# One written order on ScalarE and VectorE for the stage of the three pairs with meta tokens, with other banks and buffers

## The chip, the cores and the metric

The kernel runs on one core of a Trainium2 chip. A core has TensorE (PE in the profile, with PEld for its weight loads), VectorE (DVE), ScalarE (ACT), GpSimd (POOL) and SyncE (SP, which issues the transfers). Each engine works through its own list of instructions in order; semaphores tie the lists together. The metric is the time of one execution on the device in microseconds. The kernel before takes 1217.13 us, the median of three runs (1213.55 to 1217.62).

## The reference, cut to what matters

One block of a hybrid encoder: 1024 tokens of width 1024, with 16 learned meta tokens in front, through a norm, one wide projection `w_in`, two mixers, gates, an output projection and a squared-ReLU MLP.

```
z = u @ w_in                               # u: normed rows, meta tokens first
a, q, k, v, r, lr, ga, gb = split(z)       # widths 512, 256, 256, 512, 512, 16, 1024, 1024
p = multiscale_pool(a)                     # per group of 128: mean over 2, 4, 8 or 16 rows, minus the row
p = einsum(p, w_pool_mix) * pool_scale     # 128x128 per group
log_a = log_sigmoid(lr @ w_gate_up + b_gate) / 16
o = gla_chunked(q, k, v, log_a)            # gated linear attention in chunks of 64
m = sigmoid(ga) * (p @ w_pool_out) + sigmoid(gb) * (rmsnorm(o) * silu(r) @ w_gla_out)
```

Only `a`, `k`, `v` and `lr` are needed for the meta tokens too; that is why the stage that makes `a` and `k` works on 1040 columns and stands apart from the later projections.

## The kernel before, in words

All large products run in fp32 split in two: every operand is kept as a high part (fp32r) and a low remainder, and `mm3` (lines 285 to 287) issues high x high, high x low and low x high into the same PSUM bank. So each weight block needs a copy on ACT (the high part) and a subtraction on DVE (the low part) before PE can use it. With those three matmuls for each product PE is the busiest engine by far.

**The stage of the three pairs** is `first_products` (from line 750). A *pair* is two blocks of 128 columns of `w_in`: pair 0 is groups 2 and 3 of `a`, pair 1 groups 0 and 1, pair 2 is `k`. A pair is computed by a seven-product scheme (P1 to P7 on sums of blocks, as in Strassen's method), so the stage has 21 products; their order is the list `ORDER_2` (line 744), and n below is the place in it (n = 0 is P1 of pair 0, n = 20 is P3 of pair 2). For each n the loop issues the product (`product`, line 823), then the split of the weights for product n + 4 into one of four slots (`ready_for`, line 755; lines 789 and 790 are its ACT copy and DVE subtraction), and then what the table `beside` names for that place. Sums of weight blocks are made by POOL (line 673). Results leave PSUM through `put` and `copy` (lines 819 and 820).

PSUM has eight banks: tag `sc` (two banks, products of pairs 0 and 2), `gs` (two banks, pair 1), `y2` (two banks, always taken as one buffer) and `z` (two buffers of one bank). `two("sc")` and `two("gs")` give the same tile each time, while each `two("y2")` and `bank("z")` takes the next buffer of its pool and so waits until the last user has been read out.

**The work beside the products** is threefold.
- `lr_turn` (line 414), at n = 0: the low-rank columns `lr` (16 for each row of tokens) are transposed by PE, 16x16 for the meta tokens into a `z` bank and four 128-row blocks each into the first and the second half of `gs`. `stacked` copies each to two places on ACT (lines 416, 417) and writes the remainder on DVE (418).
- `decays(p)` (line 618), for each half of the heads: two matmuls (621) into `y2`, then Identity, Abs, Exp and Ln on ACT and one step on DVE over 1024 columns (609 to 616), in the buffers `c` (two of its four) and `dt`, an Exp (625) and a store to `decay_dram` (626). The same follows for the 16 meta columns (630) into the small tile `metab`.
- `mix_sums(g)` and `mix_products(g)`: the pooling sums of group g on DVE (645, 648) in the two `s` buffers, the split of the mixed rows into `ph` (649 on ACT, 650 on DVE), six matmuls with the 128x128 mixing weight (285 to 287 in `ph,mw`), a scaled copy out (658) into the same `s` buffer, and a store to `pm_dram` (659). They run for groups 2, 3, 1, 0.

Two things outside matter here. The **meta state** (`meta_state`, lines 1131 to 1141) uses `metab`: small DVE steps and one ACT Exp for each p, and loads of `metab` from `k_dram` (1136) that need the meta columns of `k` to be stored (817). And the **next stage**, `pairs_of_projections`, frees the right stack of SBUF (`right.pop_to(0)`) and pushes its own tiles, `fs` first: so `fs` (128 x 2 x 512) takes the memory that `dt` (128 x 2 x 512, the first tile pushed by this stage) had. POOL writes the weight sums for the fourth product of that stage (P5 of its first pair) into `fs` (line 984).

**What sets the order.** PE, POOL and SP instructions, and ACT and DVE instructions outside the first stage, are put in order by the tile framework's scheduler, from its own estimates; `tc.keep_in_program_order` pins single ones. The first stage is already written out by hand inside `tc.manual_schedule(engines={ACT, DVE, SP})`. SP issues every transfer of the main queue in one list, and a transfer whose data are not ready holds back those behind it.

Of the kernel before, what the change touches and what calls it, by code (L numbers as in the profile page):

```python
# [10 lines left out]
ACT = mybir.ActivationFunctionType  # L11
# [111 lines left out]
def kernel(  # L123
# [30 lines left out]
    def bank(tag):  # L154
        if tag == "sc":
            sc_n[0] += 1
            return two("sc")[:, sc_n[0] % 2]
        return psp[tag].tile([P, 512], F32, name=f"b_{tag}", tag=tag)

    def two(tag):  # L160

        if tag in ("sc", "gs"):
            if tag not in wide:
                wide[tag] = psp[tag].tile([P, 2, 512], F32, name=f"b_{tag}", tag=tag)
            return wide[tag]
        return psp[tag].tile([P, 2, 512], F32, name=f"b_{tag}", tag=tag)
# [247 lines left out]
    def lr_turn():  # L414
        def stacked(to, b):
            act.activation(to[:16], b, ACT.Copy)
            act.activation(to[64:80], b, ACT.Copy)
            dve.tensor_tensor(to[32:48], b, f32(to[:16]), ALU.subtract)

        b = bank("z")  # L420
        pe.transpose(b[:16, :16], S["lrtok"][:16, 8], ident[:16, :16])
        stacked(S["lr"][:, SEQ : SEQ + META], b[:16, :16])
        for h, c in enumerate(halves()):
            b = two("gs")[:, h]
            for t in range(4):
                pe.transpose(b[:16, t * P : (t + 1) * P], S["lrtok"][:, 4 * h + t], ident)
            stacked(S["lr"][:, c], b[:16])
# [190 lines left out]
    def decays(p):  # L618
        b, up = two("y2"), S["gu"][:, p * P : (p + 1) * P]
        for half, c in enumerate(halves()):  # L620
            pe.matmul(b[:, half], up, S["lr"][:, c], start=True, stop=True)
        y, t = S["c"][:, :2], S["dt"]
        yield from log_decay(b, y, t, p)
        yield
        act.activation(y, y, ACT.Exp, scale=1.0 / TAU)
        nc.sync.dma_start(decay_dram[p].rearrange("h p t -> p h t"), y)
        if p:
            act.activation(gnorm, gnorm, ACT.Copy, scale=0.5)
        b = two("y2")[:, 0, :META]
        pe.matmul(b, up, S["lr"][:, SEQ : SEQ + META], start=True, stop=True)  # L630
        for _ in log_decay(b, metab[:, META_LOG[p]], metab[:, 4], p):
            pass
        if p:
            tc.keep_in_program_order(act.preload_act_table_set("exp_and_others"))

    pooled = {}

    def mix_sums(g, eng=dve):
        a, w, e = pooled[g], WINDOWS[g], SEQ + META
        cur, k = a, 1  # L640
        while k < w:
            c = META - (w - 2 * k)
            dst = nxt("s")
            for lo, hi in ((c, e),) if eng is dve else ((c, HALF), (HALF, e)):
                eng.tensor_tensor(dst[:, lo:hi], cur[:, lo:hi], cur[:, lo - k : hi - k], ALU.add)
            cur, k = dst, 2 * k
        pp = S["pp"] = nxt("s")
        dve.scalar_tensor_tensor(pp[:, :SEQ], cur[:, META:e], 1.0 / w, a[:, META:e], ALU.mult, ALU.subtract)
        act.activation(S["ph"][:, 0], pp[:, :SEQ], ACT.Copy)
        dve.tensor_tensor(S["ph"][:, 1], pp[:, :SEQ], f32(S["ph"][:, 0]), ALU.subtract)  # L650

    def mix_products(g, tag):
        wb = (S["mw"][:, 0, g], S["mw"][:, 1, g])
        b = two(tag)
        for h, c in enumerate(halves()):
            mm3(b[:, h], 1, lambda i: wb, lambda i: (S["ph"][:, 0, c], S["ph"][:, 1, c]))
        o = S["pp"][:, :SEQ].rearrange("p (h c) -> p h c", h=2)
        act.activation(o, b, ACT.Copy, scale=pscale[:, g : g + 1])
        nc.sync.dma_start(pm_dram[g].rearrange("h p t -> p h t"), o)

# [89 lines left out]
    def first_products(wb):  # L750
# [4 lines left out]
        def ready_for(n):  # L755

            if n >= len(ORDER_2):
                if n > len(ORDER_2):
                    S["first"].append(next(S["pw"]))
                return  # L760
            p, i = ORDER_2[n]
            hi, lo = slots[(0, 2, 1, 3)[n % 4]]
            if i == 0 and p in ("P1", "P2"):
                return
            if i == 0:
                a = S["sums"][p]
            else:
                a11, a12, a21, a22 = (first_raw[i, u][:, k : k + 4] for u in range(2) for k in (0, 4))
                f, s, s5 = quad(fs), quad(s3), quad(S["c"][:, 3])
                if p == "P1":  # L770
                    a = a11
                    in_halves(s5, a21, a22, ALU.add)
                elif p == "P2":
                    a = a12
                elif p == "P6":
                    a = f
                    in_halves(f, s5, a11, ALU.subtract)
                elif p == "P5":
                    a = s5
                    in_halves(s, a11, a21, ALU.subtract)  # L780
                elif p == "P7":
                    a = s
                elif p == "P4":
                    a = a22
                else:
                    a = f
                    in_halves(f, a12, f, ALU.subtract)
            hi, lo = quad(hi), quad(lo)
            act.activation(hi, a, ACT.Copy)
            dve.tensor_tensor(lo, a, f32(hi), ALU.subtract)  # L790
# [74 lines left out]
        def mixing_weights():  # L865
            r = nxt("s")[:, :HALF]
            nc.sync.dma_start(r.rearrange("p (g e) -> p g e", g=4), w_pool_mix.rearrange("g c e -> c g e"))
            r = r.rearrange("p (g e) -> p g e", g=4)
            tc.keep_in_program_order(act.activation(S["mw"][:, 0], r, ACT.Copy))
            dve.tensor_tensor(S["mw"][:, 1], r, f32(S["mw"][:, 0]), ALU.subtract)  # L870

        ready_for(1)
# [5 lines left out]
        S["ph"] = right.push("ph", [P, 2, SEQ], F32R)  # L878
        S["mw"] = right.push("mw", [P, 2, 4, P], F32R)
        S["first"] = []  # L880
        logs = iter(())
        beside = {
            0: lr_turn,
            6: lambda: (mixing_weights(), mix_sums(2)),
            9: lambda: (mix_products(2, "y2"), mix_sums(3)),
            13: lambda: (mix_products(3, "y2"), mix_sums(1)),
            17: lambda: (mix_products(1, "gs"), mix_sums(0)),
            20: lambda: mix_products(0, "gs"),
        }
        for n in range(len(ORDER_2)):  # L890
            product(n)
            ready_for(n + 4)
            if n == 6:
                for u in range(2):
                    load_pair_block(2, u)
            if n == 11:
                first_pair()
            beside.get(n, lambda: None)()
            if n in (3, 10):
                logs = decays(n // 10)  # L900
            next(logs, None)

    step(one, first_products, W1, [w_cols(FIRST[0])])

# [1009 lines left out]
```

## Time and profile before

| | |
|---|---|
| median of three runs | 1217.13 us (1213.55 to 1217.62) |
| the profiled execution | 1217.57 us, of which the span from first to last instruction is 1215.8 us |
| mean granted TensorE clock | 0.994 of full |
| PE busy | 1192.8 us, 98% of the span |
| DVE, ACT, POOL busy | 853.9, 579.1 and 103.5 us |

Times inside the execution count from the start of the span. The stage of the three pairs runs from about 73 us (its first product) to about 156 us (the first product of the next stage). In a row of the timeline stand the start, the duration, engine, line, operation, output and inputs with their shapes; in square brackets stands how long the engine had been idle before and what released it. A row of the waits says who waited for what: total us, times, the longest. A row of the stretches gives, for each engine, the busy time in a stretch, and then the granted PE clock, the share of the transfer engines and their rate. Consecutive matmuls overlap in the records, so PE's pace is read from start to start.

### The profile page before, as it was taken

How to read it: one execution, taken by the hardware profiler on the slowest of the kernel's cores; microseconds unless marked ns; L12 is line 12 of the kernel's file. 1: busy time of each engine (PE TensorE's matmuls, PEld its weight loads, DVE VectorE, ACT ScalarE, POOL GpSimd, SP SyncE). 2: the span in 40 equal slices, each digit the busy share in tenths (PEclk: the TensorE clock that was granted, in tenths of full speed). 3: DMA queues.
4: the chain of work that ended last, by engine and by line, in shares of the span. 5: the costliest groups of instructions: out<-in, count | busy, mean ns of one | idle time of the engine just before them, and what ended most of it. 6: DMA issues, size and time to landing. Idle time of an engine off the chain costs nothing.

```text
span 1215.8 us, 18350 instructions
## 1 busy us (share of the span) xinstructions
PE 1192.8 (98%) x6775; PEld 991.2 (82%) x6775; DVE 853.9 (70%) x1392; ACT 579.1 (48%) x1006; POOL 103.5 (9%) x121
## 2 busy tenths in 40 slices
PE   9988999999999999999999999999999999999997
PEld 7978888777788888788878888888888888888886
DVE  6666856665677569725887667676675887887686
ACT  7546544444456224314655455454454444444544
POOL 0223233323320000000000000000000000000000
PEclk9989999999999999999999999999999999999999
DMA  8232343435347977911245444454479973332532
GB/s 245 65 79 87 105 116 121 147 105 164 98 140 240 342 241 245 317 51 70 104 140 168 145 163 156 130 164 146 167 243 315 337 241 101 96 98 93 174 95 87
DMA packets 151001, 192.79 MB, mean 159 GB/s; under 512 B 12088, under 2 KB 85616, under 8 KB 150912
## 3 DMA queue, kind: packets, MB, share of 16 engines
q1 hardware_dynamic: 150752, 191.56, 48.6%
q8 instruction: 53, 0.87, 0.3%
q14 instruction: 36, 0.29, 0.1%
q10 hardware_dynamic: 160, 0.07, 0.0%
HBM read 128.66 MB, written 62.93 MB: 158 GB/s over the span
## 4 chain that ended last, share of the span: by engine, by line
PE 67%; DVE 3%; DMA 1%; issue 1%; ACT 1%; SPq 0%; DVEq 0%
PE b_oa L287 5%; PE b_oa L286 5%; PE b_oa L285 5%; PE b_y L285 4%; PE b_y L287 4%; PE b_y L286 4%; PE b_mm L285 4%; PE b_mm L287 4%; PE b_mm L286 4%; PE b_ob L287 4%; PE b_ob L286 4%; PE b_ob L285 4%; PE b_z L286 3%; PE b_z L285 3%; PE b_z L287 3%; PE b_sc L285 2%
## 5 line engine op out<-in xcount | busy, mean ns | idle before, releaser
L285 PE MATMUL b_z<-th,w1h 128*128 128x512 f32 x240 | 95.7, 399 | 0.0
L286 PE MATMUL b_z<-tl,w1h 128*128 128x512 f32 x240 | 94.5, 394 | 0.4 <-DVE tl L1583 0.4
L287 PE MATMUL b_z<-th,w1l 128*128 128x512 f32 x240 | 94.2, 393 | 0.0
L285 PE MATMUL b_sc<-th,w1h 128*128 128x512 f32 (+1 forms) x232 | 89.8, 387 | 0.5 <-ACT u2p L1697 0.5
L948 ACT ACTIVATE w1h<-raw 128x512 fp32r<-128x512 f32 x103 | 64.0, 622 | 53.4 <-PE b_y L286 23.1
L286 PE MATMUL b_sc<-tl,w1h 128*128 128x512 f32 (+1 forms) x232 | 89.3, 385 | 0.0
L287 PE MATMUL b_sc<-th,w1l 128*128 128x512 f32 (+1 forms) x232 | 88.9, 383 | 0.0
L948 ACT ACTIVATE w1h<-fs 128x512 fp32r<-128x512 f32 x81 | 51.1, 631 | 66.8 <-PE b_y L286 34.9
L949 DVE TENSOR_TENSOR w1l<-raw,w1h 128x512 fp32r<-128x512 f32 x103 | 70.7, 688 | 16.5 <-ACT w1h L948 16.5
L949 DVE TENSOR_TENSOR w1l<-fs,w1h 128x512 fp32r<-128x512 f32 x81 | 56.3, 695 | 20.8 <-ACT w1h L948 20.7
L948 ACT ACTIVATE w1h<-bt 128x512 fp32r<-128x512 f32 x46 | 29.1, 632 | 70.9 <-issue 43.9
L1773 DVE TENSOR_TENSOR bt<-w,w 128x512 f32<-128x512 f32 x80 | 54.6, 683 | 1.0 <-DMA w<-in_w_ff_dram 0.9
L286 PEld LDWEIGHTS b_z<-tl,w1h 128*128 128x128 f32 x240 | 45.8, 191 | 10.3 <-DVE tl L1583 0.8
L285 PEld LDWEIGHTS b_z<-th,w1h 128*128 128x128 f32 x240 | 45.8, 191 | 10.2 <-issue 0.4
L287 PEld LDWEIGHTS b_z<-th,w1l 128*128 128x128 f32 x240 | 45.7, 190 | 10.0
L285 PEld LDWEIGHTS b_sc<-th,w1h 128*128 128x128 f32 x232 | 43.5, 188 | 10.2 <-ACT u2p L1697 1.0
L287 PEld LDWEIGHTS b_sc<-th,w1l 128*128 128x128 f32 x232 | 43.6, 188 | 8.9
L286 PEld LDWEIGHTS b_sc<-tl,w1h 128*128 128x128 f32 x232 | 43.6, 188 | 8.6
L285 PE MATMUL b_mm<-wo,th 128*128 128x512 f32 x128 | 50.4, 394 | 0.0
L287 PE MATMUL b_mm<-wo,tl 128*128 128x512 f32 x128 | 49.9, 390 | 0.0
L286 PE MATMUL b_mm<-wo,th 128*128 128x512 f32 x128 | 49.8, 389 | 0.0
L285 PE MATMUL b_y<-wo,w1h 128*128 128x512 f32 x128 | 49.8, 389 | 0.0
(513 smaller groups left out, 3402.9 us busy)
## 6 DMA issues: line engine op xcount, KB each, us to landing
hf_dram<-h SPq DMA_DIRECT2D x112, 256.0 KB, 2.1
raw<-hf_dram SPq DMA_DIRECT2D x112, 256.0 KB, 2.6
w<-in_w_ff_dram SPq DMA_DIRECT2D x64, 256.0 KB, 4.8
raw<-in_w_in_dram SPq DMA_DIRECT2D x18, 512.0 KB, 4.7
raw<-in_w_ff_dram SPq DMA_DIRECT2D x16, 512.0 KB, 4.1
rawx<-in_w_ff_dram SPq DMA_DIRECT2D x16, 512.0 KB, 4.0
rawp<-in_w_in_dram SPq DMA_DIRECT2D x14, 512.0 KB, 4.3
xs<-in_x_dram SPq DMA_DIRECT2D x8, 512.0 KB, 4.8
```

Source lines behind the costliest of these rows:

```text
L285: pe.matmul(ps, ah, bh, start=first and i == 0, stop=False, skip_group_check=more)
L286: pe.matmul(ps, ah, bl, start=False, stop=False, skip_group_check=more)
L287: pe.matmul(ps, al, bh, start=False, stop=last and i == n - 1, skip_group_check=more)
L948: act.activation(hi, a, ACT.Copy)
L949: dve.tensor_tensor(lo, a, f32(hi), ALU.subtract)
L1773: dve.tensor_tensor(bt, w, S["w2"][q[3:]][:, i], ALU.add if q[2] == "+" else ALU.subtract)
```

## The change

The ACT and DVE instructions of the stage are put inside `tc.manual_schedule`, so that they stand in the order in which the loop issues them; the table `beside` is rewritten to say after which product each step goes. To make such a table possible, `decays` yields once more (between the Exp with its store and the meta columns), and the split of the mixed rows leaves `mix_sums` for a function `mix_parts` of its own. Two single pins are dropped. Four places change what memory a step uses:
- `lr_turn` puts the 16x16 transpose into `y2`, the first four blocks into a `z` bank and only the second four into `gs`;
- `mix_products` copies its result into `dt` instead of the `s` buffer of the sums, so the four stores to `pm_dram` read `dt`;
- the loads of pair 2 are issued by the table (n = 6), and the first loads of the next stage too (n = 11), at the places where they were.

```
-        b = bank("z")
+        b = two("y2")[:, 0]
         pe.transpose(b[:16, :16], S["lrtok"][:16, 8], ident[:16, :16])
...
-            b = two("gs")[:, h]
+            b = two("gs")[:, 0] if h else bank("z")
...
         nc.sync.dma_start(decay_dram[p].rearrange("h p t -> p h t"), y)
+        yield
...
-            tc.keep_in_program_order(act.preload_act_table_set("exp_and_others"))
+            act.preload_act_table_set("exp_and_others")
...
+    def mix_parts():
+        pp = S["pp"]
         act.activation(S["ph"][:, 0], pp[:, :SEQ], ACT.Copy)
         dve.tensor_tensor(S["ph"][:, 1], pp[:, :SEQ], f32(S["ph"][:, 0]), ALU.subtract)
...
-        o = S["pp"][:, :SEQ].rearrange("p (h c) -> p h c", h=2)
+        o = S["dt"]
         act.activation(o, b, ACT.Copy, scale=pscale[:, g : g + 1])
         nc.sync.dma_start(pm_dram[g].rearrange("h p t -> p h t"), o)
...
-            0: lr_turn,
-            6: lambda: (mixing_weights(), mix_sums(2)),
-            9: lambda: (mix_products(2, "y2"), mix_sums(3)),
...
+            0: (lr_turn,), 3: (log(0),), 4: (log(0), mixing_weights), 5: (log(0),), 6: (log(0), sums(2), more_loads),
+            7: (log(0),), 8: (mix_parts,), 9: (log(0),), 10: (products(2, "y2"), sums(3)), 11: (mix_parts, first_pair),
+            12: (log(1),), 13: (log(1),), 14: (log(1),), 15: (log(1), products(3, "y2"), sums(1)),
+            16: (log(1), mix_parts, log(1)), 17: (products(1, "gs"), sums(0)), 18: (mix_parts,), 20: (products(0, "gs"),),
         }
-        for n in range(len(ORDER_2)):
-            product(n)
-            ready_for(n + 4)
...
+        with tc.manual_schedule(engines={mybir.EngineType.Activation, mybir.EngineType.DVE}):
+            for n in range(len(ORDER_2)):
+                product(n)
+                ready_for(n + 4)
+                for do in beside.get(n, ()):
+                    do()
```

Before, `decays(0)` started after n = 3 and `decays(1)` after n = 10, one step per product; the mixing went in after n = 6, 9, 13, 17 and 20. Outside the stage the order stays, apart from a few weight splits at the start of the next one. Line numbers of the changed kernel are 3 or 4 higher behind the first edits.

On PE, at the start of the stage, `lr_turn` stands behind P1 of pair 0 (`b_sc`) and ahead of P3 (`b_z<-th_140`). Before:

```order
L287 MATMUL b_sc<-th_132,w1l 128x264
L421 MATMUL b_z<-ident,lrtok 16x16
L426 MATMUL b_gs<-ident,lrtok 16x128 x8
L285 MATMUL b_z<-th_140,w1h 128x512
L286 MATMUL b_z<-tl_144,w1h 128x512
```

The same place on PE after the change (`b_y_1088` is the `y2` buffer):

```order
L287 MATMUL b_sc<-th_132,w1l 128x264
L421 MATMUL b_y_1088<-ident,lrtok 16x16
L426 MATMUL b_z<-ident,lrtok 16x128 x4
L426 MATMUL b_gs<-ident,lrtok 16x128 x4
L285 MATMUL b_z<-th_140,w1h 128x512
```

The matmuls and their places are the same; the two sets of four transposes no longer write the same tile.

On DVE, in the middle of the stage, the three sums of group 2 (645, from `a` and `s`) with their last step (648) stand among the weight splits (790). Before:

```order
L645 TENSOR_TENSOR s<-a 128x1030
L616 SCALAR_TENSOR_TENSOR c<-c,dt 128x2x512
L790 TENSOR_TENSOR w1l<-S,w1h 128x512
L819 TENSOR_TENSOR a<-t_961,b_z 128x512
L790 TENSOR_TENSOR w1l<-c,w1h 128x512
L870 TENSOR_TENSOR mw<-s,mw 128x512
L645 TENSOR_TENSOR s<-s 128x1028
L790 TENSOR_TENSOR w1l<-gB,w1h 128x512
L645 TENSOR_TENSOR s<-s 128x1024
L616 SCALAR_TENSOR_TENSOR metab<-metab 128x16
L648 SCALAR_TENSOR_TENSOR s<-s,a 128x1024
```

The same work on DVE after the change (646 and 649 are the sums, 794 a weight split, 823 the read of P2 of pair 1 out of `y2`):

```order
L794 TENSOR_TENSOR w1l<-c,w1h 128x512
L616 SCALAR_TENSOR_TENSOR c<-c,dt 128x2x512
L646 TENSOR_TENSOR s<-a 128x1030
L646 TENSOR_TENSOR s<-s 128x1028
L646 TENSOR_TENSOR s<-s 128x1024
L649 SCALAR_TENSOR_TENSOR s<-s,a 128x1024
L794 TENSOR_TENSOR w1l<-gB,w1h 128x512
L823 TENSOR_TENSOR a<-t_961,b_y_1303 128x528
L794 TENSOR_TENSOR w1l<-raw_116,w1h 128x512
L654 TENSOR_TENSOR ph<-s,ph 128x1024
```

The four sums now stand in one piece, and the read of `y2` stands behind them.

On SP, at the end of the stage, the stores of `k` (817; 128x528 for the parts with meta columns), the loads of its meta columns (1136) and the last store of the mixed rows (659) stand in this order before:

```order
L659 DMA pm_dram<-s 128x2x512
L817 DMA k_dram<-c 128x528
L1136 DMA metab<-k_dram 128x16
L118 DMA rawp_993<-in_w_in_dram 128x8x128
L817 DMA k_dram<-c 128x528
L817 DMA k_dram<-c 128x512
L1187 DMA gi<-k_dram 128x512
L1189 DMA g<-decay_dram 128x512
L659 DMA pm_dram<-s 128x2x512
L1136 DMA metab<-k_dram 128x16
L118 DMA rawp_989<-in_w_in_dram 128x8x128
```

And on SP after the change:

```order
L663 DMA pm_dram<-dt 128x2x512
L821 DMA k_dram<-c 128x528
L1139 DMA metab<-k_dram 128x16
L821 DMA k_dram<-c 128x528
L1139 DMA metab<-k_dram 128x16
L821 DMA k_dram<-c 128x512
L1190 DMA gi<-k_dram 128x512
L663 DMA pm_dram<-dt 128x2x512
L1192 DMA g<-decay_dram 128x512
L118 DMA rawp_993<-in_w_in_dram 128x8x128
```

The second load of meta columns has moved ahead of the last store of the mixed rows, and both loads of weights behind it. On POOL the sum `s3` of the next stage (line 987) now stands ahead of its first two sums `fs`, where `fs` came first before.

More of the change, by code (lines that the diff above doesn't have):

```diff
@@ L868, in mixing_weights @@
             r = r.rearrange("p (g e) -> p g e", g=4)
-            tc.keep_in_program_order(act.activation(S["mw"][:, 0], r, ACT.Copy))
+            act.activation(S["mw"][:, 0], r, ACT.Copy)
             dve.tensor_tensor(S["mw"][:, 1], r, f32(S["mw"][:, 0]), ALU.subtract)
@@ L880, in first_products, with more_loads @@
         S["first"] = []
-        logs = iter(())
-        beside = {
-            0: lr_turn,
-            6: lambda: (mixing_weights(), mix_sums(2)),
-            9: lambda: (mix_products(2, "y2"), mix_sums(3)),
-            13: lambda: (mix_products(3, "y2"), mix_sums(1)),
-            17: lambda: (mix_products(1, "gs"), mix_sums(0)),
-            20: lambda: mix_products(0, "gs"),
-        }
-        for n in range(len(ORDER_2)):
-            product(n)
-            ready_for(n + 4)
[L893 to L901, printed above, removed]
+        logs = [decays(p) for p in range(2)]
+        log = lambda p: lambda: next(logs[p], None)
+        sums, products = (lambda g: lambda: mix_sums(g)), (lambda g, tag: lambda: mix_products(g, tag))
+        def more_loads():
+            for u in range(2):
+                load_pair_block(2, u)
+        beside = {
+            0: (lr_turn,), 3: (log(0),), 4: (log(0), mixing_weights), 5: (log(0),), 6: (log(0), sums(2), more_loads),
+            7: (log(0),), 8: (mix_parts,), 9: (log(0),), 10: (products(2, "y2"), sums(3)), 11: (mix_parts, first_pair),
+            12: (log(1),), 13: (log(1),), 14: (log(1),), 15: (log(1), products(3, "y2"), sums(1)),
+            16: (log(1), mix_parts, log(1)), 17: (products(1, "gs"), sums(0)), 18: (mix_parts,), 20: (products(0, "gs"),),
+        }
+        with tc.manual_schedule(engines={mybir.EngineType.Activation, mybir.EngineType.DVE}):
[4 more added lines that the diff above has]
+                    do()
     step(one, first_products, W1, [w_cols(FIRST[0])])
```

## The prediction

> **What bounds the kernel now.** The page comes first: PE is busy nearly all the time, so a change can only give what PE waits for or runs slowly for.
>
> ```profile
> span 1215.8 us, 18350 instructions
> PE 1192.8 (98%) x6775; PEld 991.2 (82%) x6775; DVE 853.9 (70%) x1392; ACT 579.1 (48%) x1006; POOL 103.5 (9%) x121
> ```
>
> Next, the waits of PE between 40 and 160 us; they all lie in the stage that the change rewrites.
>
> ```profile
> PE b_gs L426 <- DVE lr L418: 3.5, 1, 3.5
> PE b_y L285 <- DVE a L819: 1.5, 1, 1.5
> PE b_y L285 <- ACT ph L649: 1.4, 1, 1.4
> PE b_y L286 <- DVE ph L650: 1.3, 1, 1.3
> PE b_y L285 <- ACT metab L609: 1.2, 1, 1.2
> PE b_sc L285 <- ACT t L820: 0.8, 1, 0.8
> ```
>
> They sum to 9.7 us. Third, the stretches show the granted clock (the number behind the POOL column):
>
> ```profile
> 75.00:80.00 5.00, 1.78 (x15) 1.28 (x13) 4.97 (x6) 3.21 (x8) 3.08 (x3) 0.88 0.66 164
> 80.00:85.00 5.00, 4.77 (x14) 3.65 (x15) 0.85 (x2) 1.17 (x2) 2.73 (x4) 0.50 0.10 31
> 85.00:90.00 5.00, 5.00 (x38) 4.82 (x37) 1.66 (x3) 1.27 (x2) 0.00 (x0) 0.94 0.01 3
> ...
> 130.00:135.00 5.00, 4.54 (x14) 3.65 (x15) 3.83 (x4) 1.77 (x3) 2.14 (x2) 0.66 0.03 7
> ```
>
> After the first wait, and after the two of `ph` together, PE runs at half clock for a while. Busy time lost so: 4.77 x 0.50 + 5.00 x 0.06 + 4.54 x 0.34 = 4.2 us. A restart also loses the overlap of two matmuls:
>
> ```profile
> 100.63 0.28 PE L287 MATMUL b_gs<-th,w1l 128*128 128x264 f32 x1
> 101.70 0.40 PE L285 MATMUL b_sc<-t2h,w1h 128*128 128x264 f32 x1 [0.79 <-ACT t L820]
> ```
>
> Here 0.79 us idle, but at the usual spacing of 0.12 (24 matmuls in the 2.94 us of a product, below) the second would have started at 100.75, so 0.95 went: 0.16 more, six times 1.0. In all the stage holds 9.7 + 4.2 + 1.0 = 14.9 us; that is the most the change can give.
>
> **The change part by part.** PE's own pace sets the time between events, and these groups the steps on the other engines (mean ns of one):
>
> ```profile
> 85.90 0.28 PE L285 MATMUL b_y<-th,w1h 128*128 128x264 f32 x1
> 88.84 0.28 PE L285 MATMUL b_sc<-t0h,w1h 128*128 128x264 f32 x1
> 151.65 0.39 PE L285 MATMUL b_z<-th,w1h 128*128 128x512 f32 x1
> 154.37 0.39 PE L285 MATMUL b_gs<-ph,mw 128*128 128x512 f32 x1
> ...
> L820 ACT ACTIVATE t<-b_sc 128x528 f32<-128x528 f32 x6 | 3.6, 592 | 0.0
> L789 ACT ACTIVATE w1h<-raw 128x512 fp32r<-128x512 f32 x4 | 2.5, 628 | 4.3 <-PE b_sc L286 2.6 <-PE b_z L286 1.7
> L649 ACT ACTIVATE ph<-s 128x1024 fp32r<-128x1024 f32 x4 | 4.2, 1058 | 3.7 <-DVE s L648 3.6
> L658 ACT ACTIVATE s<-b_y,small 128x1024 f32<-128x1024 f32 x2 | 2.2, 1116 | 4.5 <-PE b_y L287 4.5
> L645 DVE TENSOR_TENSOR s<-a 128x1030 f32<-128x1030 f32 (+3 forms) x4 | 4.9, 1223 | 0.0
> L650 DVE TENSOR_TENSOR ph<-s,ph 128x1024 fp32r<-128x1024 f32 x4 | 5.1, 1268 | 0.3 <-ACT ph L649 0.3
> L790 DVE TENSOR_TENSOR w1l<-raw,w1h 128x512 fp32r<-128x512 f32 x4 | 2.7, 685 | 2.2 <-ACT w1h L789 2.2
> L790 DVE TENSOR_TENSOR w1l<-gB,w1h 128x512 fp32r<-128x512 f32 x2 | 2.4, 1216 | 0.0
> L984 POOL TENSOR_TENSOR fs<-rawp 128x256 f32<-128x256 f32 x2 | 2.8, 1428 | 5.5 <-DVE c L616 5.5
> ```
>
> A product over 528 columns takes 2.94 us, over 512 columns 2.72, a mixing product half of that, 1.36.
>
> *Banks in `lr_turn`.* The second four transposes no longer wait until ACT and DVE have read the first: the 3.5 us go, and the half clock behind them. What is late next is P2 of pair 0, which needs the `y2` buffer that the 16x16 transpose now holds. DVE reads it where it read the `z` bank before, at 79.41, 0.16 long:
>
> ```profile
> 76.17 0.60 PE L426 MATMUL b_gs<-ident,lrtok 128*16 128x128 f32 x4
> ...
> 79.41 0.16 DVE L418 TENSOR_TENSOR lr<-b_z,lr 16x16 fp32r<-16x16 f32 x1
> ```
>
> The first four transposes start at 76.17 and take 0.60, the second four as long; P3 takes 2.72, and P2 is due at about 79.8. Cost nothing; each us that DVE is later would cost one.
>
> *The written order.* ACT no longer holds PE's copies behind an Exp that itself waits (0.8), and the meta columns of the first decay go behind P6 of pair 1, so P2 does not wait for their Identity (1.2). The first two mixings come one and two products later than before, and their sums and splits do not, so both are ready (1.5, 1.4 and 1.3 go). Three new waits come out of the written order:
> - The meta columns take `y2` after DVE has read P2 of pair 1, and that read stands behind four sums. From the end of P4 of pair 0: copy 0.59, four sums 4.89, a split 0.69, the read at about 0.7, together 6.9; PE fills it with two products, 5.9. Wait 1.0.
> - The second meta columns need `y2` back from the mixing of group 3, whose ACT copy waits for DVE's step on `dt`. From the end of P6 of pair 2: copy 0.59, split 0.63, Ln about 1.06 (as the 1024-column copy), step on `dt` about 1.22 (as a sum), copy out 1.12, together 4.6; PE has the mixing and P5, 4.1. Wait 0.5.
> - The mixing of group 1 follows the same step: 3.5 up to it, two sums and their last step 3.67, `ph` 1.06 and 1.27, together 9.5; PE has 1.36 + 2.72 + 0.5 + 2.9 = 7.5. Wait 2.0.
>
> None of these groups was on PE's path before, so their sizes are uncertain by some tenths each, more where POOL runs beside (1216 against 685 ns for the same split). Sum of the new waits 3.5. Gain inside the stage 14.9 - 3.5 = 11.4 us.
>
> *Nothing* comes from the dropped pins (inside the written order they have no work left), the moved scaling of four columns on ACT, or the loads of pair 2 that now stand behind the mixing weights on SP: they are needed five products later. The Exp of the meta state stands in ACT's row behind DVE's sums of group 3, and behind it a copy that P4 of pair 1 needs; I take about 1 us of margin, and each us beyond it would cost one.
>
> *`dt` for the mixed rows.* DVE's sums no longer wait until a store has read the `s` buffer; that was no wait of PE. But `dt` is the memory of `fs`, and POOL needs `fs` for the fourth product of the next stage. Before, `dt` was last used by the second decay, and POOL began `fs` at 126.48, released by DVE's step on it (616); now it must wait for the last store of mixed rows, which SP issues behind the second load of meta columns. The rows of POOL and SP before, and the sizes of the transfers (KB, us to landing; the first two of `pm_dram` are single ones, the third their median with two in the stretch):
>
> ```profile
> 126.48 2.81 POOL L984 TENSOR_TENSOR fs<-rawp 128x256 f32<-128x256 f32 x2 [5.55 <-DVE c L616]
> ...
> 149.65 0.33 SPq L817 DMA_DIRECT2D k_dram<-c  x1
> 154.08 0.33 SPq L1136 DMA_DIRECT2D metab<-k_dram  x1
> ...
> 157.91 0.41 SPq L659 DMA_DIRECT2D pm_dram<-s  x1
> ...
> pm_dram<-s SPq DMA_DIRECT2D x1, 512.0 KB, 2.7
> pm_dram<-s SPq DMA_DIRECT2D x1, 512.0 KB, 5.4
> ...
> pm_dram<-s SPq DMA_DIRECT2D x2, 512.0 KB, 4.2
> ...
> k_dram<-c SPq DMA_DIRECT2D x2, 264.0 KB, 4.7
> k_dram<-c SPq DMA_DIRECT2D x2, 256.0 KB, 3.2
> ...
> L673 POOL TENSOR_TENSOR S<-c,raw 128x256 f32<-128x256 f32 x2 | 1.4, 744 | 8.8 <-DVE w1l L790 8.8
> ...
> 164.44 0.40 PE L285 MATMUL b_z<-th,w1h 128*128 128x512 f32 x1
> ```
>
> In the times of before (11.4 us to be taken off all): the first k store goes at 149.65 and holds back the load of meta columns to 154.08; the second k store follows at about 154.5, and as the second load now waits for its landing (4.7), SP goes on at 159.2; a store, a load and then the mixed rows, at about 0.5 each, go at 160.6 instead of 157.9. Landing 4.2: 164.8. POOL makes the sum in 1.5 (two halves at 744 ns; 2.8 in the row of `fs` above, where DVE worked beside), the split takes 0.63 + 0.69: 167.6. PE wants it at 164.44. Wait about 3.2, and with the lower split of 1.22 beside POOL and the handoffs about 4.0. Ends: 2.0 where the store lands in 2.7 (its fastest in the stage), 6.6 where it takes 5.4 and POOL 2.8. I take 4.0, as most rows stand in the middle. A wait of that size halves the clock: the two drops above cost 4.2 together, so about 2.0.
>
> [...]
>
> **The sum.** 1217.57 (1215.8 of span and 1.8 around it) - 11.4 + 4.0 + 2.0 = 1212.2; the median lies 0.4 below the profiled execution: 1211.8 us.
>
> **The rivals.** A measurement of this kernel can tell 0.3% (3.7 us) from no change, so the bounds are 1213.5 and 1220.8.
> - *The wait for `fs` is hidden*: the two k stores land fast and the mixed rows leave at once. For it: a 256 KB store of k took 3.2 in the median. Against: both of 264 KB took 4.7, and the order on SP is fixed. Time 1217.1 - 11.4 = 1205.7. [...] Chance 0.15.
> - *The clock holds through that wait*: only the 4.0 is paid. 1209.7. Chance 0.12, as both drops of before followed smaller or equal waits.
> - *The written order costs more inside the stage*: ACT and DVE can no longer go round a late step, the wait of 2.0 before the mixing of group 1 halves the clock too (2.0), and the small ones grow by 1: 1214.8. Chance 0.16.
> - *Slower*: the `fs` wait repeats. The fifth product's sum is made from `fs` after the fourth's split, and the ninth's after that; if POOL runs at its contended 2.8 and the store lands in 5.4 or more, PE waits 6.6, then 2.5 and 2.5, with half clock in each gap (2.0 x 3): 17.6 in place of 6.0. It decides against the change from 11.4 on, and gives 1223. Against: before, POOL's sums took 0.7 to 1.4 us a half, and one stage's waits would have to exceed all that the other had. Chance 0.07.
>
> **How the numbers follow.** The forecast, 1211.8, has 0.50; by the ends of the `fs` wait (2.0 to 6.6) it spans 1209 to 1214.5. The range runs from the first rival to the third and a little over, 1205.3 to 1215.8, which leaves out the slower case and the edges. Faster by over 0.3% (below 1213.5): 0.8 of the forecast, the two rivals ahead and a quarter of the third, 0.71. Within 0.3%: the rest of these and a little of the slower case, 0.24. Slower: 0.05.
>
> **What would show it.** In the profile after: no wait of the second transposes, and a clock of 1.00 from 75 to 90; waits of 0.5 to 2 us before the 16-column matmuls and the mixing of group 1; the first product of the next stage at about 144.7; then POOL's `fs` released by the store of `pm_dram`, and a PE wait of 2 to 7 us at the fourth product with the clock down behind it. If POOL's `fs` starts before that product is due, or the stage still waits over 6 us inside, the forecast is wrong.

## The result, and the profile after

The changed kernel takes **1209.45 us** in the median (1208.91 to 1210.50, 5 runs), beside 1217.13 (1213.55 to 1218.10) of the kernel before on the same chip: a ratio of 0.9945 [0.9927, 0.9962], so 0.6% faster. The forecast was 1211.8. The profiled execution took 1210.5 us, 7.1 less than that of before.

The page of the changed kernel, its head and its first line by engine:

```profile
span 1208.6 us, 18340 instructions
PE 1190.7 (99%) x6775; PEld 989.3 (82%) x6775; DVE 856.7 (71%) x1392; ACT 578.3 (48%) x1006; POOL 103.6 (9%) x121
```

The waits of PE between 40 and 200 us, which is the rewritten stage and the first six products of the next one (total, times, longest, in us):

```profile
PE b_y L631 <- DVE a L823: 1.8, 1, 1.8
PE b_gs L286 <- DVE ph L654: 0.8, 1, 0.8
PE b_z L287 <- DVE w1l L952: 0.5, 1, 0.5
PE b_y L631 <- ACT dt L662: 0.5, 1, 0.5
PE b_z L285 <- DVE c L1072: 0.4, 1, 0.4
PE b_gs L285 <- ACT ph L653: 0.3, 1, 0.3
```

All six of before are gone. Those of 1.8, 0.5 (`dt`) and 0.8 + 0.3 are the three waits that the prediction foresaw inside the stage (1.0, 0.5 and 2.0 there). The 0.5 on `w1l` is the one for `fs` in the next stage, and the 0.4 behind it, at line 1072, was not foreseen. The three stage waits and the `fs` wait in PE's timeline, and a first row from the opening, long before the change:

```profile
5.76 3.75 PE L487 MATMUL b_mm<-us,ident 128*128 128x128 f32 x16 [0.52 <-DMA us<-in_norm_mix_dram]
...
106.91 0.28 PE L631 MATMUL b_y<-lr,gu 96*128 96x16 f32 x1 [1.77 <-DVE a L823]
...
130.83 0.28 PE L631 MATMUL b_y<-lr,gu 96*128 96x16 f32 x1 [0.53 <-ACT dt L662]
...
135.63 0.50 PE L286 MATMUL b_gs<-ph,mw 128*128 128x512 f32 x1 [0.77 <-DVE ph L654]
...
156.60 0.49 PE L287 MATMUL b_z<-th,w1l 128*128 128x512 f32 x1 [0.54 <-DVE w1l L952]
```

The length of the stage, from its first product to the first product of the next, in the stretches of before and of after (us, PE busy, granted clock, DMA share, GB/s):

```profile
73.05:156.10 83.05, 73.27 (x473) 0.94 0.31 91
```

```profile
74.63:146.82 72.19, 68.78 (x473) 1.00 0.36 107
```

The stage is 10.9 us shorter, and its clock is full in this execution. It also began 1.6 us late. 0.4 of that is a wait for a transfer (the row at 5.76; before, the same matmuls went without a wait at 5.38); the rest is pace, since those 16 matmuls take 3.75 us here and 2.83 before, and the six behind them 3.40 and 2.74. That is no work of the change, as the other runs below show. So the profiled difference is made of -10.9 in the stage, +1.6 from the opening and +2.1 behind the stage.

The `fs` wait was forecast at 4.0 us, because two stores of `k` and one of mixed rows stand ahead of POOL's sum. SP's row in the same profile (start, us), and POOL's sum:

```profile
141.00 0.33 SPq L821 DMA_DIRECT2D k_dram<-c  x1
144.53 0.33 SPq L1139 DMA_DIRECT2D metab<-k_dram  x1
144.95 0.38 SPq L821 DMA_DIRECT2D k_dram<-c  x1
147.17 0.32 SPq L1139 DMA_DIRECT2D metab<-k_dram  x1
...
148.53 0.41 SPq L663 DMA_DIRECT2D pm_dram<-dt  x1
...
152.70 1.90 POOL L987 TENSOR_TENSOR fs<-rawp 128x256 f32<-128x256 f32 x2 [10.30 <-DMA g<-decay_dram]
```

The sequence is as forecast: each load of meta columns goes only when the store of `k` ahead of it has landed, and the mixed rows go behind both. But the two stores took 3.5 and 2.2 us from issue to the load behind them, where 4.4 and 4.7 were put. POOL's row names the load of `g` (1192) as its releaser, but that was issued at 149.00 and took 4.0 to land, so it landed at 153.0, after POOL had begun. The mixed rows, issued at 148.53, landed 3.9 later, at 152.4, which fits the start at 152.70; the prediction had put 4.2 for them.

### The profile page after: what moved, and what is told of

It reads as the page before. It is cut to its first block, busy times and chain, and to the rows that moved or that the text cites. A ratio compares the mean times of both kernels' runs of the same rounds, so it can differ in the third digit from the quotient of the medians.

```text
span 1208.6 us, 18340 instructions
## 1 busy us (share of the span) xinstructions
PE 1190.7 (99%) x6775; PEld 989.3 (82%) x6775; DVE 856.7 (71%) x1392; ACT 578.3 (48%) x1006; POOL 103.6 (9%) x121
## 4 chain that ended last, share of the span: by engine, by line
PE 68%; DVE 3%; issue 1%; DMA 1%; ACT 1%; SPq 0%; DVEq 0%
PE b_oa L285 5%; PE b_oa L287 5%; PE b_oa L286 5%; PE b_y L285 4%; PE b_y L287 4%; PE b_y L286 4%; PE b_mm L285 4%; PE b_mm L287 4%; PE b_mm L286 4%; PE b_ob L285 4%; PE b_ob L286 4%; PE b_ob L287 4%; PE b_z L286 3%; PE b_z L287 3%; PE b_z L285 3%; PE b_sc L285 2%
## 5 line engine op out<-in xcount | busy, mean ns | idle before, releaser
L952 DVE TENSOR_TENSOR w1l<-bt,w1h 128x512 fp32r<-128x512 f32 x46 | 31.8, 691 | 25.9 <-ACT w1h L951 25.9
```

## The experiments

Three spans of each profiled execution tell most of it: the start of the first product (P1) of the stage, the length of the stage, and the time from the first product of the next stage to the start of the last matmul. They are read from PE's timelines. The last two columns are of the timed runs; the ratios are against the kernel before, timed on the same chip. The experiments ran on three chips, on which the kernel before took 1216.23, 1216.83 and 1216.83 us in the median.

| kernel | P1 at | stage | rest | median us (range) | ratio |
|---|---|---|---|---|---|
| before | 73.05 | 83.05 | 1051.6 | 1217.13 (1213.55 to 1218.10) | |
| changed | 74.63 | 72.19 | 1053.7 | 1209.45 (1208.91 to 1210.50) | 0.9945 [0.9927, 0.9962] |
| banks only | 72.19 | 77.11 | 1051.8 | 1209.65 (1208.83 to 1211.02) | 0.9946 [0.9929, 0.9963] |
| old banks | 72.97 | 77.41 | 1055.4 | 1214.74 (1213.34 to 1215.70) | 0.9990 [0.9980, 0.9999] |
| `dt` last | 72.37 | 73.80 | 1051.9 | 1208.79 (1207.97 to 1209.62) | 0.9938 [0.9921, 0.9955] |
| mixed rows in `s` | 72.33 | 78.48 | 1051.7 | 1213.01 (1212.22 to 1214.51) | 0.9974 [0.9964, 0.9984] |
| changed, again | 73.32 | 73.79 | 1054.2 | 1209.30 (1208.15 to 1211.26) | 0.9939 [0.9918, 0.9960] |
| later steps | 72.42 | 72.55 | 1052.9 | 1207.88 (1207.71 to 1208.16) | 0.9926 [0.9904, 0.9949] |
| later, `dt` last | 72.58 | 73.20 | 1052.4 | 1208.53 (1208.11 to 1209.70) | 0.9933 [0.9913, 0.9952] |
| sums late | 72.37 | 73.81 | 1054.5 | 1210.78 (1210.65 to 1211.23) | 0.9950 [0.9931, 0.9969] |
| columns first | 72.56 | 71.99 | 1053.1 | 1206.40 (1206.30 to 1207.57) | 0.9924 [0.9903, 0.9946] |
| both columns | 72.94 | 73.60 | 1052.5 | 1208.93 (1207.17 to 1209.96) | 0.9941 [0.9919, 0.9964] |
| sums later | 72.62 | 72.25 | 1058.3 | 1213.99 (1213.00 to 1216.57) | 0.9984 [0.9971, 0.9996] |

### The banks alone, and the rest without the banks

The kernel before with only the three banks of `lr_turn` changed:

```
-        b = bank("z")
+        b = two("y2")[:, 0]
...
-            b = two("gs")[:, h]
+            b = two("gs")[:, 0] if h else bank("z")
```

> The kernel before with the three other banks in lr_turn and nothing else. Theory (the waits that went were separate, each worth its own idle time and the clock behind it): the wait of the second transposes (3.5) and the half clock of 80 to 86 go, about 6 us of the 10.9 that the stage gained; the other five waits and the clock drop near 130 stay. About 1211. Rival (the stage has slack that another wait takes up): the later waits grow by what the first gave, and the time stays at 1215 to 1217.

The median is that of the whole change, 1209.65. The waits of PE in its stage are those of before without the 3.5 (the two that are left out here are 1.3 and 0.8):

```profile
PE b_y L285 <- DVE a L819: 1.5, 1, 1.5
PE b_y L286 <- DVE ph L650: 1.3, 1, 1.3
PE b_y L285 <- ACT ph L649: 1.3, 1, 1.3
```

The two waits for `ph` still halve the clock behind them, in its stretches:

```profile
120.00:125.00 5.00, 2.45 (x10) 0.95 0.30 111
125.00:130.00 5.00, 5.00 (x22) 0.71 0.27 105
```

The stage is 5.9 us shorter than before: 3.5 of wait, and most of the rest the half clock behind it.

The other way round, the changed kernel with the old banks (the same lines, put back):

> The changed kernel with the three banks of lr_turn as before. Theory: the 3.5 us wait of the second transposes and the half clock behind it come back, and the rest of the stage stays as in the changed kernel: about 1209.5 + 6 = 1215.5. Rival (the written order alone carries the gain): at most 1211.

1214.74. The 3.5 is back, beside the waits of the changed kernel (these are its two longest):

```profile
PE b_gs L426 <- DVE lr L418: 3.5, 1, 3.5
PE b_y L631 <- DVE a L823: 1.8, 1, 1.8
```

But the half clock behind the 3.5, which the expectation had as well, did not come back in this profile. PE began again at 80.15 and ran at full clock:

```profile
70.00:80.00 10.00, 6.70 (x55) 1.00 0.55 143
80.00:90.00 10.00, 9.85 (x68) 1.00 0.24 68
```

So a wait of 3.5 us in one and the same place halved the clock in the profile of before and left it up in this one. The stage here is 5.6 us shorter than before. The two parts nearly add up in the stage: 5.9 + 5.6 = 11.5, and the whole change gave 10.9 in one profile and 9.3 in the other, with the clock in a different state in each. But the rest of the change (the order and `dt`, without the banks) costs 2.1 to 3.8 us behind the stage (rest of 1053.7, 1054.2 and 1055.4 against 1051.6), and the banks cost 0.2 there. By the profiles it adds 3.3 to 4.9 to the banks in the stage (77.11 less 73.79 or 72.19) and gives back about 2; in the medians nothing of it is left that can be measured: 1209.65 with the banks alone, 1209.45 and 1209.30 with everything.

### The memory of `fs`, and the buffer of the mixed rows

The changed kernel with `dt` laid out behind the mixing weights, so that `fs` does not lie on it:

```
-        S["dt"] = right.push("dt", [P, 2, HALF], F32)
         buffer("a", 2, SEQ + 2 * META, right)
...
         S["mw"] = right.push("mw", [P, 2, 4, P], F32R)
+        S["dt"] = right.push("dt", [P, 2, HALF], F32)
```

> The changed kernel with dt pushed behind mw in place of first, so that fs no longer takes the memory of dt. Theory (fs waits for the last store of mixed rows): fs is made some 10 us earlier, the 0.5 us wait at the fourth product of the next stage goes with what it costs around it, 1.1 us, and the time is about 1208.3. Rival (the fourth product is late for another reason, such as its place in ScalarE's row): the wait stays at 0.5 and the time at 1209.5.

1208.79. POOL begins `fs` at 139.85 in place of 152.70. Both waits in the next stage go, the 0.5 for `fs` and the 0.4 of line 1072. The second does not simply hang on the first, since it stands without it in the kernel with later steps below. The rest is 1051.9 again, 1.9 less than in the profile after. This is what sharing the memory costs here: 1.9 us, where 6.0 were forecast. (SP's row changes too in this kernel: a load of weights moves ahead of the second load of meta columns.) Yet the median is only 0.7 lower. In its profile the clock fell behind the first wait of the stage, which it had not done in the profile after:

```profile
105.00:110.00 5.00, 5.00 (x16) 0.68 0.17 41
```

The changed kernel with the mixed rows back in the `s` buffer:

```
-        o = S["dt"]
+        o = S["pp"][:, :SEQ].rearrange("p (h c) -> p h c", h=2)
```

> The changed kernel with the mixed rows copied into the s buffer of the sums, as before. Theory (two costs against each other): the wait for fs goes, 1.1 us, but VectorE's sums wait again until a store has read the s buffer (2.2 us before), and the waits of PE for the mixing grow by 1 to 3 us: 1209 to 1212. Rival (the s buffers are free in time because the mixing comes later): 1208.3, as with dt in another place.

1213.01, slower than any case of the expectation. The rest is that of before, but DVE's sums now wait for a store to read `s` (4.1 us in two waits, and 3.1 more at line 649), and the written order leaves them no way round it: a new wait ahead of the mixing of group 1, with half clock behind it:

```profile
PE b_gs L285 <- ACT ph L653: 4.3, 1, 4.3
```

```profile
135.00:140.00 5.00, 3.37 (x8) 0.54 0.00 0
140.00:145.00 5.00, 5.00 (x34) 0.78 0.41 157
```

So the order and `dt` belong together: the change without that buffer is 3.6 us worse.

### The same wait, with and without half clock

The changed kernel, unaltered, once more:

> The changed kernel once more, for a second profile of it. Theory (the wait of 1.8 us ahead of the 16 columns of the first decay halves TensorE's clock in some executions and not in others, for one and the same order): the waits are again 1.8, 0.8, 0.5, 0.5, 0.4 and 0.3 us, the median is again near 1209.5 us, and the granted clock behind the 1.8 us is either 1.00, as in the profile after, or near 0.5 for some 3 us as in the run with the old banks, with the shift against the kernel before about 2.6 us smaller there. Rival (the clock falls there only in the kernels whose code before that place differs): 1.00 again, whenever it is run.

1209.30, and the waits are the same to a tenth. The opening was late by only 0.3 us this time, but the clock fell behind the wait of 1.8. First the profile after, where PE began again at 106.91, then this one, where it began again at 105.58 and ran at full clock until 106.67:

```profile
107.00:110.50 3.50, 3.50 (x16) 1.00 0.00 0
```

```profile
107.00:110.50 3.50, 3.50 (x10) 0.56 0.15 23
```

One kernel, one wait of 1.77 and 1.78 us, and 16 matmuls in the one stretch against 10 in the other. Seven profiles of this study have this wait; the clock fell behind it in four (old banks, `dt` last, this one, sums late) and held in three (after, mixed rows in `s`, sums later). Where it fell, the stage is about 1.6 us longer (73.79 to 73.81 in three of them against 72.19 and 72.25; the other two have other waits as well).

What the traces show of the two is this. Every stretch of half clock in these stages lasts 3.41 or 6.83 us (78.75 to 85.58 and 129.95 to 133.37 before, 106.67 to 110.08 here). In the profile of before 44.37 us lie between the two stretches (85.58 to 129.95), 13 times 3.41. In the profile after the clock changes only at 10.63 and at 1205.29, which is 350 times 3.41 apart.

PE's idle time, summed in steps of 3.41 us from those times, goes with the falls in both profiles. Before, it is 1.98 us in the step that ends with the first fall (75.34 to 78.75) and 2.18 in the one that ends with the second (126.54 to 129.95); in every other step at full clock up to 1195 us it is 1.15 or less. After, where the clock held, it is 1.11 or less: the wait of 1.77 is cut into 1.06 and 0.71 there (at 106.20).

Laid out the same way from the times at which their clock changed, other profiles agree only in part. In the four where the clock fell behind the wait of 1.8, the wait lies whole in the step that ends with the fall; in sums later, where the clock held, the wait is cut into about 1.05 and 0.73. But in mixed rows in `s` it lies in one step but for 0.1 us at most, and the clock held. The 3.5 of old banks is cut into about 1.7 and 1.8, and the clock held there too. No run was made to test whether the place decides.

### The steps one product later

The prediction's first and third wait, with their steps moved:

```
-            7: (log(0),), 8: (mix_parts,), 9: (log(0),), 10: (products(2, "y2"), sums(3)), 11: (mix_parts, first_pair),
+            7: (log(0),), 8: (mix_parts,), 10: (products(2, "y2"), sums(3)), 11: (log(0), mix_parts, first_pair),
...
-            16: (log(1), mix_parts, log(1)), 17: (products(1, "gs"), sums(0)), 18: (mix_parts,), 20: (products(0, "gs"),),
+            16: (log(1), mix_parts, log(1)), 18: (products(1, "gs"), sums(0)), 19: (mix_parts,), 20: (products(0, "gs"),),
```

> The changed kernel with three steps asked for one or two products later: the fourth part of the first decay with its 16 columns (behind product 11 in place of 9, so behind DVE's read of P2), the products of the mixing of group 1 (18 in place of 17) and the next parts of mixed rows (19 in place of 18). Theory (the waits of 1.8 and of 0.8 + 0.3 us come from the places of these steps alone, and the first also costs a half clock of about 2.6 us in part of the executions): the 1.8 and the 0.8 + 0.3 us are gone, a median of 1205.5 to 1207.5 us. Rival (VectorE and ScalarE are late in this stretch wherever the steps stand, so the waits come back at the next product): waits of 2 us or more in all remain, 1208.5 to 1210 us.

1207.88, faster than the changed kernel, between the two theories. The 1.8 is gone and the clock holds, and the four timed runs lie within 0.45 us where the nine of the changed kernel spread over 3.1. But two other waits came in the middle of the stage, that for `dt` grew from 0.5 to 1.4, a wait of 0.5 came ahead of the mixing of group 0, and the 0.4 of line 1072 stayed. The three largest:

```profile
PE b_y L631 <- ACT dt L662: 1.4, 1, 1.4
PE b_y L286 <- DVE ph L654: 1.2, 1, 1.2
PE b_y L285 <- ACT metab L609: 0.6, 1, 0.6
```

The waits inside the stage sum to 3.7, no less than the 3.4 of the changed kernel, and the stage of 72.55 is no shorter than its 72.19 with full clock. What is gained is the clock, which stayed at 1.00 through the stage; its longest wait is 1.4.

The same with `dt` laid out last:

> The same three steps later, and the buffer of the mixed rows laid out so that the next stage's sums do not share its memory. Theory: the waits of the stage and those of the next stage's 4th product and of P5 of its pair 1 (0.5 and 0.4 us, 1.5 to 1.9 us of lateness) go together, since they do not hang on each other: 1203.5 to 1206.5 us, 1 to 2 us under the kernel with the later steps alone. Rival (what is gained in the stage is lost at the next weights, which are made no sooner): within 0.5 us of the kernel with the later steps alone.

1208.53: no gain, 0.65 us slower than with the later steps alone, which is just outside the 0.5 of the rival, and for another reason. With the later steps alone the wait for `fs` was gone already and only the 0.4 of line 1072 was left; that goes here, while the mixing of group 0 waits 1.1 in place of 0.5, so that the waits sum to 4.3 against 4.1.

The 1.2 comes of the mixing of group 2, which now follows too soon on its sums. The 0.6 does not, though the expectation below takes it so: it stands at 132.74, behind the 16 columns of the second decay, 25 us later. The 16 columns of the first decay now go first and the mixing of group 2 behind the next product:

```
-            7: (log(0),), 8: (mix_parts,), 10: (products(2, "y2"), sums(3)), 11: (log(0), mix_parts, first_pair),
+            7: (log(0),), 8: (mix_parts,), 10: (log(0), sums(3)), 11: (products(2, "y2"), mix_parts, first_pair),
```

> From the kernel with the three later steps: the 16 columns of the first decay go behind product 10, ahead of the products of the mixing of group 2, and those go behind product 11. In the kernel before this one the mixing of group 2 waited 1.2 us in its middle for VectorE's half of the mixed rows, and the 16 columns, behind it on the same bank, held back 0.6 us. Theory (each wait is set by how many products stand between a step and the last VectorE instruction that it needs, and 24 matmuls of 264 columns, about 3.3 us, are enough): both waits are gone, 1.8 us less and no half clock, 1206 to 1206.8 us. Rival (VectorE has no slack there, so the read of the next product comes late and the wait moves on): 1207.5 us or more.

**1206.40**, the fastest of all, 3.05 below the changed kernel's median with no overlap of their runs, though on another chip. By the profiles, stage and rest together are 0.8 us shorter than in the profile after, where the clock held, and 2.9 shorter than in the second one, where it fell. Its waits between 40 and 200:

```profile
PE b_y L631 <- ACT dt L662: 1.0, 1, 1.0
PE b_gs L286 <- DVE ph L654: 0.9, 1, 0.9
PE b_y L621 <- ACT dt L662: 0.7, 1, 0.7
PE b_y L285 <- ACT metab L609: 0.6, 1, 0.6
PE b_z L285 <- DVE c L1072: 0.5, 1, 0.5
```

The 1.2 is gone and the theory's time was met, but not all of its reason: the mixing's copy out now holds the matmuls of the second decay by 0.7, and the 0.6 stayed, as the second decay's columns had not moved. No wait is over 1.0, and the clock is full over the stage; two of its stretches:

```profile
110.00:120.00 10.00, 9.29 (x64) 8.49 (x63) 9.91 (x17) 4.71 (x7) 3.47 (x4) 1.00 0.27 91
120.00:130.00 10.00, 9.04 (x59) 7.96 (x58) 7.35 (x9) 8.21 (x12) 0.00 (x0) 1.00 0.52 141
```

One step further, the second decay's 16 columns behind product 17 (`16: (log(1), mix_parts), 17: (log(1),)`):

> The same, and the last part of the second decay with its 16 columns one product later (behind product 17 in place of 16), since they waited 1.4 us for ScalarE's copy of the mixing of group 3, which is itself held by VectorE's read of the buffer that the decay's rows and the mixed rows share. Theory: that wait goes as well, 1204.8 to 1205.8 us, and it is the fastest of all kernels here. Rival (the short steps on 16 columns now lie ahead of the first weights of the next stage on ScalarE and VectorE, and what is gained is lost there): within 0.5 us of the kernel without this step, or slower.

1208.93, slower than without it, as the rival had it, but not for the rival's reason: the loss is not in the next stage (rest 1052.5) but at the next product, which needs the columns' bank. ACT reads the columns only behind its split of the mixed rows (653) and a copy:

```profile
PE b_y L285 <- ACT metab L609: 2.4, 1, 2.4
```

```profile
130.94 1.06 ACT L653 ACTIVATE ph<-s 128x1024 fp32r<-128x1024 f32 x1 [1.01 <-DVE s L649]
...
132.49 0.26 ACT L609 ACTIVATE metab<-b_y,small 128x16 f32<-128x16 f32 x1
```

PE made the columns at 130.20 and waited for line 609 until 132.8. The clock fell behind that wait.

### A wait for `fs` as long as the forecast

The changed kernel with POOL making a difference in the place of its sum first, in one kernel once (without the loop), in another three times:

```
                 if p == "P5":
+                    if eng is pool and i == 0:
+                        for _ in range(3):
+                            tt(s, a21, a22, ALU.subtract)
                     tt(s, a21, a22, ALU.add)
```

> The changed kernel with GpSimd making the sum for the 4th product of the next stage twice (first as a difference that is written over), 3.3 us more by its two rows of 1.90 and 1.43 us, so that TensorE waits there about as long as the prediction had it: 0.5 + 3.3 = 3.8 us. Theory A (a wait of that length halves the clock behind it, as it did behind lr_turn): 3.3 us of wait and 1.5 to 2.5 us of half clock, 1214 to 1215.5 us. Theory B (the wait alone, with the clock held): 1212 to 1213 us. Theory C (the lateness is taken up by later slack): under 1211 us.

1210.78, and the expectation had the added work wrong: it took POOL's two rows of `fs` for one sum, but the second is the sum of pair 1. Four halves took 3.28 us here where two took 1.90, so it was 1.38 later. PE waited 1.4 + 0.5 us at full clock, so this run did not reach the disputed size, and its time, under the 1211 of theory C, does not speak for that theory.

> The changed kernel with GpSimd making the difference three times over ahead of the sum for the 4th product of the next stage. Made once, it took only 1.38 us (the row of four takes 3.28 us where that of two takes 1.90), TensorE waited 1.4 + 0.5 us there at full clock, and the kernel came to 1210.78 us. Three times: 4.2 us later than in the changed kernel, a wait of about 4.2 us ahead of the first matmul of the 4th product, as the prediction had it. Theory A (a wait of that length halves the clock behind it): 1215 to 1216.5 us, with a granted clock near 0.6 in the 5 us behind it. Theory B (the wait alone): 1213 to 1214 us at 1.00. Theory C (the following products make it up): under 1212.5 us.

1213.99. The added work was 4.1 us (6.02 for eight halves), PE waited 3.9 ahead of the 4th product, from 153.38 to 157.27, and the clock was at half from 155.36 to 162.19, the last 4.9 us of that behind the wait; the wait, then the stretch:

```profile
PE b_z L285 <- ACT w1h L951: 3.9, 1, 3.9
```

```profile
157.20:162.20 5.00, 4.88 (x11) 0.50 0.42 107
```

The half clock costs 2.4 us beside the wait: at 4.88 us of busy time and half clock PE does the work of 2.44. The rest is 1058.3, which is 6.7 above that of before and 4.6 above the profile after, and the median is 4.5 above the changed kernel's. So theory A's mechanism is shown. The median lies in theory B's range, but by chance, since the clock was not at 1.00; theory A's time was too high, because it added the whole price to a median that has about 1.9 of it already. The prediction's price for a wait of 4.0, 6.0 us with the half clock, was about right, and only the wait did not come.

## Why the prediction was right, and where its sizes were off

- *What the stage holds* (14.9 us: six waits, half clock, restarts). Right. 10.9 went and 3.4 of new waits stand in their place, 14.3 in all. Of the sum, the banks had 3.5 of wait and 2.7 of half clock. By the prediction's own terms the other steps were thus worth 14.9 - 6.2 - 3.5 = 5.2 in the stage and lost 6.0 behind it, about nothing in sum, and the medians of banks only and changed (1209.65 and 1209.45) say the same.
- *Banks in `lr_turn`*, cost nothing. Right: no wait at the second transposes and full clock behind them, and with this edit alone nothing is late in its place.
- *New waits inside the stage*, 3.5 in sum. Measured 1.8 + 0.5 + 1.1 = 3.4, and the stage gained 10.9 where 11.4 was forecast. The parts were mis-sized against each other. The wait behind P2 of pair 1 took 1.8 in place of 1.0, since DVE's four sums begin behind a step of the first decay (616) that the sum of times had left out, and take 5.5 us (100.10 to 105.63) where 4.89 were put, 1.76 of it for the first. DVE's timeline of the profile after:

```profile
98.53 1.64 DVE L616 SCALAR_TENSOR_TENSOR c<-c,dt 128x1024 f32<-128x1024 f32 x1 [0.25 <-ACT dt L615]
100.10 1.76 DVE L646 TENSOR_TENSOR s<-a 128x1030 f32<-128x1030 f32 x1
101.89 2.49 DVE L646 TENSOR_TENSOR s<-s 128x1028 f32<-128x1028 f32 x2
104.41 1.22 DVE L649 SCALAR_TENSOR_TENSOR s<-s,a 128x1024 f32<-128x1024 f32 x1
...
106.16 0.70 DVE L823 TENSOR_TENSOR a<-t,b_y 128x528 f32<-128x528 f32 x1
```

- *No half clock inside the stage.* This step failed in part. The forecast put none behind the wait of 1.0; it came as one of 1.8 that halves the clock in some executions, about 1.6 us each time. Nor did every long wait halve it: the 3.5 of old banks did not. For a wait of 4.0 the forecast put 2.0 of half clock, and the 3.9 of sums later cost 2.4.
- *`dt` shares memory with `fs`*, 4.0 + 2.0. The mechanism was right (SP's row, POOL's start, the wait at the 4th product, all gone with `dt` elsewhere), the size was not: 1.9 in place of 6.0. The mis-sized term is the landing of the stores of `k`, 4.4 and 4.7 against 3.5 and 2.2 measured. The price was read from a place where the store had company. SP's row of before:

```profile
154.51 0.39 SPq L118 DMA_DIRECT2D rawp<-in_w_in_dram  x1
154.98 1.77 SPq L817 DMA_DIRECT2D k_dram<-c  x2
...
160.11 0.32 SPq L1136 DMA_DIRECT2D metab<-k_dram  x1
```

The second store stood 0.5 us behind a 512 KB load of weights there, with another store of `k`, and took 5.1 to the load of meta columns; after, it goes alone and takes 2.2. That the company is the cause was not isolated. The two landings were put 3.4 us too high, and with them the wait came out at 0.5 in place of 4.0, with the clock at 1.00 behind it. The whole term is 4.1 us too high, more than the 2.35 us by which the forecast was too slow; the stage, 0.5 short, and the half clock just named lie on the other side. That the total came out nearer than its largest new term is in part luck.
- *The rivals.* A hidden `fs` wait (1205.7): nearest to what happened in the next stage, but not hidden. The clock that holds: it did hold there, behind a wait of 0.5; a wait of 3.9 in that place brought the clock down. The written order costing more: the mixing's wait came at 1.1. Slower: the later sums did not hold PE; behind the 0.5 came only the 0.4 of line 1072, DVE's read of a `z` bank.

What stays open: by the profiles the order should gain 1.0 to 3.0 us over the banks alone with all its costs (stage and rest together 1128.9 against 1127.9 and 1125.9), and the medians show 0.2 to 0.35. Openings that differ by 2.4 us between executions (P1 at 72.19 to 74.63) and the clock that falls or not (1.6 us) are of that size or larger, and four to nine runs do not separate them.

## What to carry to other kernels

Split a change into its parts before crediting it: here three bank names gave all of the measured gain, and an order written by hand, though it shortened its stage, added nothing that could be measured until its steps were set one product later. Look at the longest wait and not only at the sum of waits: no wait of 1.4 us or less brought the clock down by itself, and one of 1.8 did in four of seven profiles. In a written order, ask for a step only when its last input was asked for a product earlier, and look at what takes the bank next, since a step moved later can hold the product behind it, as the 2.4 us did. Do not carry a transfer's duration to another place without the load around it.

## What the runs showed of the hardware that was not expected

- The same wait of PE, 1.77 to 1.78 us in the same place, halves the granted clock in four profiles and not in three, for 3.4 us each time. A longer wait did not always do it: the 3.9 did when it was 2.0 us old (153.38 to 155.36), and the 3.5 of old banks did not.
- The clock fell ten times in the stages and the products behind them. Ahead of the falls PE waited 3.5 us (before), 1.4 and 1.3 close together (before), twice 1.3 (banks only), 1.77 to 1.78 (old banks, `dt` last, changed again, sums late), 4.3 (mixed rows in `s`), 2.4 (both columns) and 3.9 (sums later).
- The half clock costs half of the time that PE works in it (in sums later a matmul of 512 columns starts every 0.43 us there, and every 0.23 at full clock): about 1.6 us behind a wait of 1.8 (3.41 us at half clock), and 2.4 behind one of 3.9 (4.9 of the 6.83 us at half clock, the rest of which was wait).
- A store of 264 KB of `k` took 4.4 and 5.1 us from issue to the load behind it before, and 3.5 and 2.2 after.
